# Hybrid decoder step on one core: whole-array products for the chunk scores and the sample tokens, and decays as biases of the exponentials

## The chip, the cores and the metric

The kernel runs on one core of one Trainium2 chip. The metric is the device time of one execution in microseconds. The core's engines work side by side and each takes its own instructions in order: TensorE (PE: matrix products; its weight loads are listed apart as PEld), VectorE (DVE), ScalarE (ACT), GpSimd (POOL), and SyncE (SP), which here only issues transfers. SBUF is the on-chip memory, PSUM the small one in banks of 128 partitions x 512 fp32 that PE writes to.

## The reference, cut to what matters

One layer of a decoder trunk: RMSNorm, one input projection, two groups of heads side by side, one output projection, residual, RMSNorm. 1024 new tokens ("prompt") start from an empty state; 8 sequences of 4 tokens ("sample") start from given states. The group that the change touches is the gated linear recurrence with four heads of 128 keys and 128 values:

```python
def step(s, inp):
    qb, kb, vb, gb = inp
    g = jnp.cumsum(gb, axis=2)                     # summed log of the forget gates
    diff = g[:, :, :, None, :] - g[:, :, None, :, :]
    decay = jnp.exp(jnp.where(causal, diff, -jnp.inf))
    scores = jnp.einsum('nhtd,nhsd,nhtsd->nhts', qb, kb, decay)
    o = (jnp.einsum('nhts,nhsv->nhtv', scores, vb)
         + jnp.einsum('nhtd,nhdv->nhtv', qb * jnp.exp(g), s))
    g_last = g[:, :, -1:, :]
    s_new = (jnp.exp(g_last[:, :, 0, :])[..., None] * s
             + jnp.einsum('nhsd,nhsv->nhdv', kb * jnp.exp(g_last - g), vb))
    return s_new, o
```

Here `k = 1 - f`, `gb = log(f)`, `f = lb + (1 - lb) * sigmoid(...)`. The output of each head goes through an RMSNorm and is gated with `silu(za)`. The other group is a gated depthwise convolution of width 31 with LayerNorm; it runs mostly on DVE.

## The kernel before, in words

Activations lie transposed: 128 channels on the partitions, 1056 tokens (1024 prompt, 32 sample) along the free dimension. `emit` walks over a list `order` of 24 blocks of 128 output channels. For each, `load_w` fetches the weights, ACT rounds them into a high part `wh` and DVE takes the low part `wl`; `project` multiplies them in three column blocks of 352, each with 24 matmuls into one of four `mm` banks. ACT or DVE then empties the banks (`evac`), ACT after a load of the table for the sigmoid or SiLU. All calls on PE and DVE are recorded with one line, L72, since they go through the helper `Clock`.

The recurrence of head `hd` is the generator `hgrn`. It is queued when its q block is projected, and `pump` takes steps from it, and from the convolution's generator `conv`, between the column blocks of later projections. A scheduler then sets the final order on each engine from these priorities and a simulated timeline. The recurrence's small matmuls therefore stand among the projections' on PE, and the convolution's multiply-adds fill DVE.

For the prompt, `hgrn` runs in two halves of 512 tokens, each of four chunks of 128. `base` (L511) subtracts, on DVE, the summed gate at the middle of each chunk, takes two exponentials on ACT (L514, L515) and multiplies them with k and q on DVE. The scores of a chunk are then made in two pieces, in tiles of 64 columns of PE's array (tile names: `ptps` is the score bank, `hw` holds the products with k and q, `pt` the masked scores):

```python
T.matmul(ptps[0:64, cs], lhsT=kb[:, c * P : c1], rhs=qb[:, cs], ...)
T.matmul(ptps[64:P, c1:ce], lhsT=kb[:, c1:ce], rhs=qb[:, c1:ce], ..., tile_position=(0, 64))
```

The quarter above the diagonal is not computed; DVE clears the bank once (L974), and `masked` copies the causal part of the scores into `pt`. k is transposed on PE, copied by ACT (L532), and multiplied with the values `vt` for the state (`aux<-vt,ho`); `ops` takes scores times values plus queries times state. `head_norm` normalizes.

For the sample tokens of each head, `hgrn` lays the decayed keys out four times (`k4`, tile `kts`), transposes them, repeats the head's 32 value rows on four groups of partitions by a product with a constant matrix (`aux<-vs,bones`, 32 rows of the array), forms the 32 x 32 scores from a second set of exponentials in a tile of 32 columns (`aux<-sm`), masks them into `ptss`, and multiplies them with the 32 value rows (`ops<-pts,vs`, 32 rows). `aux<-raw,qz` and `aux<-hw,kts` are the products with the old and for the new states; `raw` holds the state, read and written by SP's queue.

If the decays were too strong for the factored form, a flag that is computed on the way starts a second, slower program (`fast=False`). It does not run on this data.

Of the kernel before, what the change touches and what calls it, by code (L numbers as in the profile page):

```python
# [21 lines left out]
NB = 8  # L22
NS = 4
ST = NB * NS
# [3 lines left out]
H = 4  # L28
# [4 lines left out]
EPS = 1e-6  # L33
LB_MIN = 0.02
RANGE = 60.0
VPOS = 4
LEAD = 10.0
HU = 3
# [7 lines left out]
C_HG = 0  # L46
# [10 lines left out]
NMASK = 2 + len(LEVELS)  # L57
# [39 lines left out]
def emit(nc, tc, h, fast, flag_out=None):  # L97
    HW = 5
    with ExitStack() as ctx:
# [5 lines left out]
        def sb(shape, tag, bufs=1, dt=F32):  # L105
            return pool.tile(shape, dt, tag=tag, name=tag, bufs=bufs)
# [18 lines left out]
        make_identity(nc, ident)  # L125
        eps = sb([P, 1], "eps")
        nc.vector.memset(eps, EPS)
        avgr = sb([P, P], "avg", dt=F32R)
        avg = avgr.bitcast(F32)
        av = sb([P, P], "st", 5)  # L130
# [9 lines left out]
        vs = sb([P, P], "vs")  # L140
# [182 lines left out]
        cols = sb([P, C_END], "cols")  # L323
# [29 lines left out]
        ptss = sb([P, ST], "pts")  # L353
        nc.gpsimd.memset(ptss, 0.0)


        lb = sb([P, 4], "lb")
        omlb = sb([P, 4], "omlb")
        nomlb = sb([P, 4], "nomlb")
# [11 lines left out]
        V.tensor_scalar(nomlb, lb, -1.0, None, ALU.add)  # L371
        if fast:
            rng = sb([P, H, 16], "rng")
        wsum = sb([P, 60], "wsum")
# [87 lines left out]
        def hgrn(hd, q, k, g):  # L462
# [4 lines left out]
            if fast:  # L467

                gc = g[:, 0:SEQ].rearrange("p (c t) -> p c t", t=P)
                r0, r1 = rng[:, hd, 0:8], rng[:, hd, 8:16]  # L470
                V.tensor_copy(r0, gc[:, :, P // 2 - 1])
                V.tensor_tensor(r1, gc[:, :, P - 1], r0, ALU.subtract)

                eg = sb([P, 9], "eg", 2)
                V.tensor_tensor(eg[:, 1:8], r0[:, 1:8], r1[:, 0:7], ALU.add)
                V.tensor_copy(eg[:, 8:9], r1[:, 7:8])
                S.activation(eg[:, 1:9], eg[:, 1:9], AF.Exp)
            for hf in range(2):
# [32 lines left out]
                def base(blk, idx, src=gv, n=512, mk=hw, qq=qv, kk=kv):  # L511
                    d = rel(blk, idx, src, n, mk)
                    kb = mk()
                    S.activation(kb, d, AF.Exp, scale=-1.0)  # L514
                    S.activation(d, d, AF.Exp)  # L515
# [7 lines left out]
                if fast:  # L523


                    qb, kb = base(P, P // 2 - 1)
                    yield
                    kps = aux()
                    for c in range(4):
# [2 lines left out]
                    S.copy(kT, kps)  # L532
                    for c in range(4):
                        cs = slice(c * P, (c + 1) * P)
                        c1, ce = c * P + P // 2, c * P + P

                        T.matmul(
                            ptps[0:64, cs], lhsT=kb[:, c * P : c1], rhs=qb[:, cs],
                            start=True, stop=True,
                        )  # L540
                        T.matmul(
                            ptps[64:P, c1:ce], lhsT=kb[:, c1:ce], rhs=qb[:, c1:ce],
                            start=True, stop=True, tile_position=(0, 64),
                        )
                    for pr in range(2):
                        masked(
                            pts[pr],
# [116 lines left out]
                        stop=True,  # L664
                    )
                yield
                yield from head_norm(hd, c0, 512, ops)
            if fast:
                end = sb([P, P], "st", 5)
                V.tensor_scalar(end, st, eg[:, 8:9], None, ALU.mult)  # L670
                st = end
            nc.sync.dma_start(h["o_hp"][hd], st)
            yield
# [13 lines left out]
            k4 = sb([P, 4, ST], "kts", 3)  # L687
            V.tensor_tensor(
                k4,
                ki.unsqueeze(1).to_broadcast([P, 4, ST]),  # L690
                kv.unsqueeze(1).to_broadcast([P, 4, ST]),
                ALU.mult,
            )
# [16 lines left out]
            for dst, src, r0, r1 in ((kT, 0, 2, 4), (vr, P, 1, 2), (vr, P, 3, 4)):  # L710
                rr = slice(r0 * ST, r1 * ST)
                V.tensor_tensor(
                    dst[rr], kps[rr, src : src + P], dst[rr].bitcast(F32), ALU.subtract
                )
            qi = sm()
            S.activation(qi, gv, AF.Exp)
            qz = qzs[0]
# [4 lines left out]
                ALU.mult,  # L722
            )
            yield
            sps = aux()
            if fast:
                qb, kb = base(NS, 1, gv, ST, sm, qv, kv)
                pairs = [(kb, qb)]
            else:
# [5 lines left out]
            for i, (a, b) in enumerate(pairs):  # L735
                sp = sps[rows, i * ST : (i + 1) * ST]
                T.matmul(sp, lhsT=a, rhs=b, start=True, stop=True, tile_position=(0, hd * ST))
                mi = 0 if fast else NMASK - 3 + i
                V.copy_predicated(ptss[rows, :], smask[rows, mi, :], sp)
            ops = bank("ops", 1)  # L740
            T.matmul(
                ops[:, 0:ST],
                lhsT=vs[rows, :],
                rhs=ptss[rows, :],
                start=True,
                stop=False,
                tile_position=(hd * ST, 0),
            )
            ips = aux()
            for b in range(NB):  # L750
# [6 lines left out]
                    stop=(b >= 4),  # L757
                    tile_position=(0, j * ST),
                )
            isb = sb([P, P], "kts", 3)  # L760
            S.copy(isb, ips[:, 0:P])
            T.matmul(ops[:, 0:ST], lhsT=isb, rhs=bones[:, 0:ST], start=False, stop=True)
            yield
# [20 lines left out]
                    )  # L784
            nc.sync.dma_start(h["o_hs"][hd], so)
            yield
            yield from head_norm(hd, SEQ, ST, ops)
            hdone.add(hd)

        def head_norm(hd, c0, n, ops):  # L790
# [8 lines left out]
            S.activation(r, ms[:, 0:n], AF.Ln, bias=eps)  # L799
            S.activation(r, r, AF.Exp, scale=-0.5)  # L800
            V.scalar_tensor_tensor(
                r, ops[:, 0:n], cols[:, C_HG : C_HG + 1], r, ALU.mult, ALU.mult
            )
            yield

# [161 lines left out]
        for i, (kind, c) in enumerate(order):  # L967
            if i == VPOS:
                t0 = T.ns
                for tb in range(2, 8):  # L970
                    v_block(tb)
                T.ns = t0
                ptps = bank("ptps", 1)
                V.memset(ptps, 0.0)  # L974
                late["ptps"] = ptps
                mixa = late["mixa"] = big()
            if i + 1 < len(order):
# [29 lines left out]
            elif kind == "f":  # L1007
# [2 lines left out]
                project(w, act_into(kt, AF.Sigmoid), nd)  # L1010
                S.activation(g, kt, AF.Ln, bias=lb[:, c : c + 1], scale=omlb[:, c : c + 1])
                S.activation(
                    kt, kt, AF.Identity, bias=omlb[:, c : c + 1], scale=nomlb[:, c : c + 1]
                )
                for hf in range(4):
                    gs = g[:, hf * 256 : hf * 256 + 256]
# [339 lines left out]
```

## Time and profile before

| | us |
|---|---|
| time, median of 3 runs (lowest, highest) | 500.35 (499.99, 501.29) |
| the profiled execution's own time | 500.03 |
| its span, first to last instruction | 498.2 |
| PE busy in the span | 484.2 |
| DVE busy | 358.6 |
| ACT busy | 250.6 |
| PE's granted clock, mean | 0.993 |

By place in the span: up to about 133 us x is normed and transposed, the values of all tokens and the first blocks are projected. From 133 to about 372 us the recurrence of the four heads runs among the projections. From there to 403 come the last gate blocks and LayerNorm, then the output projection up to 489, and the last rows' norm and write.

A row of the timeline has: start in us, length in us, engine, line, operation, output tile <- input tiles, active rows * columns of the array, shape, count, and in brackets the idle time before. Rows of one kind that follow one another are merged, and a row's length reaches to the end of its last matmul, which overlaps the next row; so the distance between starts is the time that something takes on PE.

### The profile page before, as it was taken

What the parts mean: (1) busy time and instruction counts of PE and PEld (TensorE: products, weight loads), DVE (VectorE), ACT (ScalarE), POOL (GpSimd) and SP (SyncE); (2) the same over time, 40 slices, a digit from 0 to 9 for tenths busy, and PEclk for the clock granted to TensorE, in tenths of its full rate; (3) what the DMA queues carried; (4) which work ended last, traced back from release to release, by engine and by line L of the source; (5) the groups of instructions that cost most, each with busy time, mean ns of one, the idle gap of its engine ahead of it and who ended that gap; (6) DMA issues with size and microseconds to landing.
All of it is one profiled execution on the core that took longest, in us unless ns stands there. A gap on an engine that the chain in (4) does not pass through costs nothing.

```text
span 498.2 us, 7600 instructions
## 1 busy us (share of the span) xinstructions
PE 484.2 (97%) x3020; PEld 442.7 (89%) x3020; DVE 358.6 (72%) x682; ACT 250.6 (50%) x439; POOL 3.0 (1%) x20
## 2 busy tenths in 40 slices
PE   6999999999999999999999999999999999999992
PEld 5788899999999998999999999999999977877781
DVE  4864213999999989998999988993677747543441
ACT  5764332413646554635536554545766985422321
POOL 1000000000000000000000000000000000000000
PEclk9999999999999999999999999999999999999997
DMA  7910501231111213211123101131115396432111
GB/s 272 314 43 13 170 25 30 42 62 36 42 44 43 52 49 61 88 43 43 48 55 128 27 27 49 42 128 44 47 43 180 89 415 202 153 114 86 42 53 49
DMA packets 23003, 43.52 MB, mean 87 GB/s; under 512 B 10640, under 2 KB 11920, under 8 KB 22960
## 3 DMA queue, kind: packets, MB, share of 16 engines
q1 hardware_dynamic: 21808, 40.86, 26.3%
q10 hardware_dynamic: 1152, 2.10, 1.1%
q8 instruction: 25, 0.41, 0.3%
q14 instruction: 18, 0.15, 0.1%
HBM read 35.72 MB, written 7.24 MB: 86 GB/s over the span
## 4 chain that ended last, share of the span: by engine, by line
PE 90%; ACT 4%; DMA 3%; DVE 2%; issue 1%; SPq 0%; DVEq 0%
PE mm L72 70%; PE ops L72 8%; PE ptps L72 6%; PE aux L72 5%; DMA u<-gin 1%; ACT big L954 1%; DMA raw<-wo 1%; DMA o_hs<-raw 1%; DVE raw L72 1%; ACT L455 1%; DVE qkg L72 0%; ACT big L1100 0%; DVE big L72 0%; ACT qkg L455 0%; DVE u L72 0%
## 5 line engine op out<-in xcount | busy, mean ns | idle before, releaser
L72 PE MATMUL mm<-big,wh 128*128 128x352 f32 (+1 forms) x1280 | 323.7, 332 | 0.0
L72 PEld LDWEIGHTS mm<-big,wh 128*128 128x128 f32 x1280 | 224.1, 188 | 8.1 <-issue 1.6
L72 PE MATMUL mm<-big,wl 128*128 128x352 f32 (+1 forms) x640 | 211.4, 331 | 0.0
L72 PEld LDWEIGHTS mm<-big,wl 128*128 128x128 f32 x640 | 120.5, 188 | 3.4 <-issue 0.4
L72 DVE TENSOR_TENSOR wl<-wraw,wh 128x1024 fp32r<-128x1024 f32 x24 | 29.3, 1222 | 25.9 <-ACT wh L390 25.8
L72 DVE SCALAR_TENSOR_TENSOR big<-u,wsum,big 128x511 f32<-128x511 f32 (+14 forms) x60 | 44.5, 741 | 0.6
L72 DVE SCALAR_TENSOR_TENSOR big<-u,cols,big 128x511 f32<-128x511 f32 (+14 forms) x60 | 44.0, 735 | 0.0
L72 DVE SCALAR_TENSOR_TENSOR cq<-u,cols,cq 128x511 f32<-128x511 f32 (+13 forms) x56 | 41.2, 735 | 0.0
L72 DVE TENSOR_TENSOR qkg<-mm,big 128x512 f32<-128x512 f32 x16 | 10.9, 690 | 35.7 <-PE mm L72 35.7
L390 ACT CAST wh<-wraw 128x1024 fp32r<-128x1024 f32 x24 | 25.1, 1047 | 17.2 <-issue 7.8
L72 PE MATMUL mm<-vt,wh 128*128 128x512 f32 x64 | 25.6, 402 | 0.4 <-ACT wh L1167 0.4
L395 ACT ACT_TABLE_LOAD x20 | 25.7, 1283 | 0.3
L455 ACT ACTIVATE qkg<-mm 128x352 f32<-128x352 f32 x48 | 19.4, 465 | 11.4 <-PE mm L72 11.3
L72 PE MATMUL mm<-vt,wl 128*128 128x512 f32 x64 | 24.8, 390 | 0.0
L1204 ACT ACTIVATE big<-qkg 128x512 f32<-128x512 f32 x16 | 10.0, 628 | 29.1 <-DVE qkg L72 29.1
L455 ACT ACT_TABLE_LOAD x16 | 20.5, 1283 | 1.3 <-PE mm L72 1.0
L72 PE MATMUL ops<-big 128*128 128x512 f32 x64 | 20.8, 403 | 0.2 <-ACT big L197 0.2
L72 PE MATMUL ptps<-big 128*128 128x512 f32 x64 | 19.9, 394 | 0.0
L1167 ACT CAST wh<-big 128x512 fp32r<-128x512 f32 x16 | 9.2, 617 | 19.1 <-PE mm L72 18.6
L72 PEld LDWEIGHTS mm<-vt,wh 128*128 128x128 f32 x64 | 12.0, 188 | 5.2 <-ACT wh L1167 1.7
L72 PE MATMUL mm<-hw,wh 128*128 128x512 f32 x40 | 15.7, 392 | 0.0
L799 ACT ACTIVATE big<-aux,eps 128x512 f32<-128x512 f32 (+1 forms) x12 | 6.7, 556 | 17.9 <-PE aux L72 17.5
(239 smaller groups left out, 634.7 us busy)
## 6 DMA issues: line engine op xcount, KB each, us to landing
wraw<-win SPq DMA_DIRECT2D x24, 512.0 KB, 3.6
wraw<-wo SPq DMA_DIRECT2D x12, 512.0 KB, 3.7
big<-xp SPq DMA_DIRECT2D x2, 2048.0 KB, 10.1
big<-xp SPq DMA_DIRECT2D x4, 512.0 KB, 10.7
raw<-sh SPq DMA_DIRECT2D x4, 512.0 KB, 3.5
o_hs<-raw SPq DMA_DIRECT2D x4, 512.0 KB, 3.0
raw<-wo SPq DMA_DIRECT2D x4, 512.0 KB, 5.2
o_yp<-qkg ACTq DMA_DIRECT2D x8, 256.0 KB, 2.9
```

The costliest lines, as they stand in the source:

```text
L72: return f(*a, **k)
L390: S.copy(hi, wr)
L395: after(S.preload_act_table_set("natural_log_exp_and_others"), prev)
L455: return [S.activation(dst[:, nb * MB : (nb + 1) * MB], ps, func, bias=bias)]
L799: S.activation(r, ms[:, 0:n], AF.Ln, bias=eps)
L954: return S.activation(cv[:, c, cs], cv[:, c, cs], AF.Silu, bias=cols[:, C_LNB + c : C_LNB + c + 1], scale=cols[:, C_LNG + c : C_LNG + c + 1],)
L1167: S.copy(hv, m[:, :, ts])
L1204: S.activation(xr[:, hs], y[:, hs], AF.Square, accum_out=sqs[:, half : half + 1])
```

## The change

- The scores of a chunk become one whole 128 x 128 x 128 product. The part above the diagonal is computed too and masked away as before. The clearing of the bank goes.
- `base` is no longer used for the prompt. The exponentials read the summed gates directly, chunk by chunk, with the chunk's middle value (`rng`, and its negative `nm`) as the bias of the ACT instruction: 8 instructions of 128 columns per half in place of two of 512 (64 in place of 16 in all).
- k is scaled by 2^-16 where it is made (`kb0`, `kw`); the scale is taken out again in the norm (`hgk`, and a scale in the logarithm), in the final state and in the sample's `k4`.
- The sample scores use the four-fold `k4` as weights of a whole product of 32 columns, behind the transpose in the same bank, and the same exponential for q (`qe`). The scores of a head lie in a plane of their own in `ptss` (zero elsewhere), so that their product with the values is whole as well.
- The repeated value rows come by four transfers on SP's queue per head (`v4`), and are rounded by ACT from there. Tile `kts` has four buffers in place of three.

```diff
+                nm = sb([P, 8], "nm", 2)
+                V.tensor_scalar(nm, r0, -1.0, None, ALU.mult)
...
-                    qb, kb = base(P, P // 2 - 1)
+                    qb, kb = hw(), hw()
+                    for c in range(4):
+                        cs, cc = slice(c * P, (c + 1) * P), hf * 4 + c
+                        S.activation(
+                            kb[:, cs], gv[:, cs], AF.Exp, bias=r0[:, cc : cc + 1], scale=-1.0
+                        )
+                    for c in range(4):
+                        cs, cc = slice(c * P, (c + 1) * P), hf * 4 + c
+                        S.activation(qb[:, cs], gv[:, cs], AF.Exp, bias=nm[:, cc : cc + 1])
+                    V.tensor_tensor(kb, kb, kv, ALU.mult)
+                    V.tensor_tensor(qb, qb, qv, ALU.mult)
...
-                        T.matmul(
-                            ptps[0:64, cs], lhsT=kb[:, c * P : c1], rhs=qb[:, cs],
-                            start=True, stop=True,
-                        )
-                        T.matmul(
-                            ptps[64:P, c1:ce], lhsT=kb[:, c1:ce], rhs=qb[:, c1:ce],
-                            start=True, stop=True, tile_position=(0, 64),
-                        )
+                        T.matmul(ptps[:, cs], lhsT=kb[:, cs], rhs=qb[:, cs], start=True, stop=True)
...
+            v4 = sb([P, P], "kts", 4)
+            for j in range(4):
+                nc.sync.dma_start(v4[j * ST : (j + 1) * ST, :], vs[rows, :])
+            yield
...
+            if fast:
+                qe = sm()
+                S.activation(qe, ki, AF.Exp)
+                V.tensor_tensor(qe, qe, qv, ALU.mult)
...
-            T.matmul(
-                kps[:, P : 2 * P],
-                lhsT=bones[rows, :],
-                rhs=vs[rows, :],
-                start=True,
-                stop=True,
-                tile_position=(hd * ST, 0),
-            )
-            kT = sb([P, P], "kts", 3, F32R)
-            vr = sb([P, P], "kts", 3, F32R)
+            if fast:
+                sps = kps[:, P : P + ST]
+                T.matmul(
+                    sps, lhsT=k4.rearrange("p a t -> p (a t)"), rhs=qe, start=True, stop=True
+                )
+                V.copy_predicated(ptss[rows, hd, :], smask[rows, 0, :], sps[rows, :])
+            vr = sb([P, P], "kts", 4, F32R)
+            S.copy(vr, v4)
+            kT = sb([P, P], "kts", 4, F32R)
             S.copy(kT, kps[:, 0:P])
-            S.copy(vr, kps[:, P : 2 * P])
...
             T.matmul(
                 ops[:, 0:ST],
-                lhsT=vs[rows, :],
-                rhs=ptss[rows, :],
+                lhsT=vs,
+                rhs=ptss[:, hd, :],
                 start=True,
                 stop=False,
-                tile_position=(hd * ST, 0),
             )
...
-                V.memset(ptps, 0.0)
```

Since the scheduler sets the order, these rows show what moves. A row is a line, an operation, output tile <- input tiles and the output's shape; a count stands at the end. First PE at the scores of the first head's first half (`mm` is a projection, `aux<-ident,hw` the transposes of k), before and then after:

```order
L72 MATMUL aux<-ident,hw 128x128 x4
L72 MATMUL mm<-big,wh 128x352 x2
L72 MATMUL mm<-big,wl 128x352
...
L72 MATMUL ptps<-hw 64x128
L72 MATMUL ptps<-hw 64x64
...
L72 MATMUL mm<-big,wh 128x352 x2
L72 MATMUL mm<-big,wl 128x352
...
L72 MATMUL aux<-vt,ho 128x128 x4
```

```order
L73 MATMUL aux<-ident,hw 128x128 x4
L73 MATMUL mm<-big,wh 128x352
L73 MATMUL mm<-big,wl 128x352
...
L73 MATMUL mm<-big,wh 128x352
L73 MATMUL ptps<-hw 128x128 x4
L73 MATMUL mm<-big,wh 128x352
L73 MATMUL mm<-big,wl 128x352
```

Eight pieces of two widths, alternating, become four products of one shape in the same place between the projections.

PE at the first head's sample tokens, without the projections between the rows, before and after:

```order
L72 MATMUL aux<-ident,kts 128x128
L72 MATMUL aux<-vs,bones 128x128
...
L72 MATMUL aux<-sm 32x32
...
L72 MATMUL aux<-raw,qz_425 32x128 x8
...
L72 MATMUL ops<-pts,vs 128x32
L72 MATMUL aux<-hw,kts 128x512
...
L72 MATMUL ops<-bones,kts 128x32
L72 MATMUL aux<-hw,kts 128x512
```

```order
L73 MATMUL aux<-ident,kts 128x128
L73 MATMUL aux<-sm,kts 128x32
...
L73 MATMUL aux<-raw,qz_425 32x128 x8
...
L73 MATMUL ops<-pts,vs 128x32
...
L73 MATMUL aux<-hw,kts 128x512
...
L73 MATMUL ops<-bones,kts 128x32
L73 MATMUL aux<-hw,kts 128x512
```

The repeat of the value rows is gone from PE, and the score product has moved up behind the transpose; the others keep their sequence.

ACT between two emptyings of projections (`qkg<-mm`: q of the first head, then the forget gates of the second), before and after:

```order
L390 CAST wh<-wraw 128x1024
L514 ACTIVATE hw<-hw 128x512
L686 ACTIVATE sm<-sm 128x32
L514 ACTIVATE sm<-sm 128x32
L515 ACTIVATE hw<-hw 128x512
L515 ACTIVATE sm<-sm 128x32
L477 ACTIVATE eg<-eg 128x8
L532 COPY ho<-aux 128x512
L455 ACT_TABLE_LOAD
```

```order
L397 CAST wh<-wraw 128x1024
L538 ACTIVATE hw<-qkg,rng 128x128 x4
L704 ACTIVATE sm<-sm 128x32
L735 ACTIVATE sm<-qkg 128x32
L543 ACTIVATE hw<-qkg,nm 128x128 x4
L486 ACTIVATE eg<-eg 128x8
L706 ACTIVATE sm<-sm 128x32
L728 CAST kts<-kts 128x128
L538 ACTIVATE hw<-qkg,rng 128x128 x4
L543 ACTIVATE hw<-qkg,nm 128x128 x4
L462 ACT_TABLE_LOAD
```

The two wide exponentials of one half have become eight narrow ones, the second half's eight stand ahead of the same table load too, and the copy `ho<-aux` has moved behind it.

More of the change, by code (lines that the diff above doesn't have):

```diff
@@ L35 @@
 RANGE = 60.0
+KS = 2.0 ** -16
 VPOS = 4
@@ L127, in emit @@
         nc.vector.memset(eps, EPS)
+        ks = KS if fast else 1.0
         avgr = sb([P, P], "avg", dt=F32R)
@@ L352, in emit @@
         nc.sync.dma_start(bones, h["bones"])
-        ptss = sb([P, ST], "pts")
+        ptss = sb([P, H, ST], "pts")
         nc.gpsimd.memset(ptss, 0.0)
@@ L358, in emit @@
         omlb = sb([P, 4], "omlb")
-        nomlb = sb([P, 4], "nomlb")
+        kc = sb([P, 9], "kc")
+        kb0, kw, hgk = kc[:, 0:4], kc[:, 4:8], kc[:, 8:9]
         l0 = cols[:, C_LOG : C_LOG + 4]
@@ L370, in emit @@
         V.tensor_scalar(omlb, lb, -1.0, 1.0, ALU.mult, ALU.add)
-        V.tensor_scalar(nomlb, lb, -1.0, None, ALU.add)
+        V.tensor_scalar(kb0, lb, -ks, ks, ALU.mult, ALU.add)
+        V.tensor_scalar(kw, lb, ks, -ks, ALU.mult, ALU.add)
+        V.tensor_scalar(hgk, cols[:, C_HG : C_HG + 1], 1.0 / ks, None, ALU.mult)
         if fast:
@@ L666, in hgrn @@
                 yield
-                yield from head_norm(hd, c0, 512, ops)
+                yield from head_norm(hd, c0, 512, ops, ks, hgk)
             if fast:
                 end = sb([P, P], "st", 5)
-                V.tensor_scalar(end, st, eg[:, 8:9], None, ALU.mult)
+                V.tensor_scalar(end, st, eg[:, 8:9], 1.0 / ks, ALU.mult, ALU.mult)
                 st = end
@@ L724, in hgrn @@
             yield
[L725 to L729, printed above, removed]
+            if not fast:
+                sps = aux()
                 pairs = []
@@ L734, in hgrn @@
                 pairs.append((kv, qv))
[L735 to L739, printed above, removed]
+                for i, (a, b) in enumerate(pairs):
+                    sp = sps[rows, i * ST : (i + 1) * ST]
+                    T.matmul(sp, lhsT=a, rhs=b, start=True, stop=True, tile_position=(0, hd * ST))
+                    V.copy_predicated(ptss[rows, hd, :], smask[rows, NMASK - 3 + i, :], sp)
             ops = bank("ops", 1)
@@ L759, in hgrn @@
                 )
-            isb = sb([P, P], "kts", 3)
+            isb = sb([P, P], "kts", 4)
             S.copy(isb, ips[:, 0:P])
@@ L786, in hgrn, with head_norm @@
             yield
-            yield from head_norm(hd, SEQ, ST, ops)
+            yield from head_norm(hd, SEQ, ST, ops, 1.0, cols[:, C_HG : C_HG + 1])
             hdone.add(hd)
-        def head_norm(hd, c0, n, ops):
+        def head_norm(hd, c0, n, ops, ks, hg):
             lo = sb([P, 512], "ho", 2, F32R)
@@ L798, in head_norm @@
             mean(ms[:, 0:n], hi[:, 0:n], lo[:, 0:n])
-            S.activation(r, ms[:, 0:n], AF.Ln, bias=eps)
+            S.activation(r, ms[:, 0:n], AF.Ln, bias=eps, scale=1.0 / (ks * ks))
             S.activation(r, r, AF.Exp, scale=-0.5)
             V.scalar_tensor_tensor(
-                r, ops[:, 0:n], cols[:, C_HG : C_HG + 1], r, ALU.mult, ALU.mult
+                r, ops[:, 0:n], hg, r, ALU.mult, ALU.mult
             )
@@ L1012, in emit @@
                 S.activation(
-                    kt, kt, AF.Identity, bias=omlb[:, c : c + 1], scale=nomlb[:, c : c + 1]
+                    kt, kt, AF.Identity, bias=kb0[:, c : c + 1], scale=kw[:, c : c + 1]
                 )
```

13 lines of the change are left out of this document (6 added, 7 removed).

## The prediction

> **What bounds the kernel now.** I read the page's busy times first, then the chain that ended last, then the busy times by stretch. The page's engine line and the chain's shares:
>
> ```profile
> PE 484.2 (97%) x3020; PEld 442.7 (89%) x3020; DVE 358.6 (72%) x682; ACT 250.6 (50%) x439; POOL 3.0 (1%) x20
> PE 90%; ACT 4%; DMA 3%; DVE 2%; issue 1%; SPq 0%; DVEq 0%
> ```
>
> TensorE is at work almost from end to end, but its busy time is modelled and an average, so the stretches matter. Columns: stretch; us and busy us (instructions) of PE, weight loads, DVE, ACT, POOL; granted clock; DMA share; GB/s.
>
> ```profile
> 133.00:160.00 27.00, 27.00 (x186) 26.59 (x185) 25.94 (x55) 15.05 (x26) 0.00 (x0) 1.00 0.15 40
> 160.00:215.00 55.00, 55.00 (x389) 51.83 (x389) 50.90 (x102) 29.79 (x49) 0.25 (x2) 1.00 0.25 67
> 215.00:270.00 55.00, 55.00 (x374) 52.75 (x372) 52.15 (x106) 29.36 (x50) 0.00 (x0) 1.00 0.18 53
> 270.00:330.00 60.00, 60.00 (x416) 57.83 (x416) 55.25 (x108) 31.20 (x53) 0.00 (x0) 1.00 0.18 55
> 330.00:372.00 42.00, 42.00 (x295) 40.02 (x293) 26.73 (x45) 24.78 (x39) 0.00 (x0) 1.00 0.18 56
> ```
>
> All that the change touches lies between 133 and 372 us. There PE never stops and has its full clock, so a TensorE slot that goes away shortens the run by its own length, as long as nothing else takes over. DVE is the nearest: 25.94 + 50.90 + 52.15 + 55.25 = 184.2 us of the 197 up to 330, or 93.5%. ACT has 130.2 of 239 us.
>
> **Chunk scores.** PE around the first head's first half. Every fp32 product shows as two MATMULs.
>
> ```profile
> 146.50 0.32 PE L72 MATMUL mm<-big,wl 128*128 128x352 f32 x1
> 146.75 1.09 PE L72 MATMUL ptps<-hw 128*64 128x128 f32 x16
> 147.77 0.59 PE L72 MATMUL mm<-big,wh 128*128 128x352 f32 x2
> 148.20 0.32 PE L72 MATMUL mm<-big,wl 128*128 128x352 f32 x1
> 148.36 0.48 PE L72 MATMUL mm<-big,wh 128*128 128x352 f32 x2
> 148.68 0.32 PE L72 MATMUL mm<-big,wl 128*128 128x352 f32 x1
> 148.84 1.05 PE L72 MATMUL aux<-vt,ho 128*128 128x128 f32 x8
> ...
> 150.05 0.32 PE L72 MATMUL mm<-big,wl 128*128 128x352 f32 x1
> ```
>
> A projection matmul starts every 0.16 us (three from 148.20 to 148.68). The cost of a group is the time between the projection matmuls around it, less these themselves. The scores in 64-column tiles take 148.20 - 146.50 - 3 x 0.16 = 1.22 us. The group at 148.84 is four whole 128x128x128 products, exactly the shape that the scores will have: 150.05 - 148.68 - 0.48 = 0.89 us, or 0.11 per MATMUL. What the tiles lose is at their edges: the group starts 0.25 after the matmul ahead instead of 0.16, and the two behind take 0.43 instead of 0.32.
>
> The rule that speaks against this edit is in the Trainium skill, TensorEngine Tiling, section Theoretical Speedup: a dimension of 64 or less may run up to 2x faster in tiles. By that alone the whole products would cost up to twice the tiled group, an estimate of +1.22 us per half and +9.8 in all. The same page's Key Properties say that a change of tiling mode drains the array; the two gaps in the rows above agree with that.
>
> Six of the eight halves have one unbroken group and save 0.33 us each: 2.0 us. Two are broken up by whole-array work and have more edges; these are the projection matmuls around them:
>
> ```profile
> 207.36 0.32 PE L72 MATMUL mm<-big,wl 128*128 128x352 f32 x1
> 210.97 0.32 PE L72 MATMUL mm<-big,wl 128*128 128x352 f32 x1
> ...
> 332.75 0.32 PE L72 MATMUL mm<-big,wh 128*128 128x352 f32 x1
> 335.74 0.48 PE L72 MATMUL mm<-big,wh 128*128 128x352 f32 x2
> ```
>
> PE's timeline has in both the 16 score MATMULs, ten whole ones (1.11 us) and some projections. 210.97 - 207.36 = 3.61 with three projections (0.48) leaves 2.02 for the scores: 1.13 saved against 0.89. 335.74 - 332.75 = 2.99 with two (0.32) leaves 1.56: 0.67 saved. Chunk scores together: 2.0 + 1.1 + 0.7 = **-3.8 us**. In the new order some groups are again broken, but whole products among whole products have no edge.
>
> **Sample tokens.** PE in the first head's sample part:
>
> ```profile
> 184.24 0.27 PE L72 MATMUL aux<-ident,kts 128*128 128x128 f32 x1
> 184.44 0.48 PE L72 MATMUL aux<-vs,bones 32*128 32x128 f32 x2
> ...
> 185.12 0.32 PE L72 MATMUL mm<-big,wl 128*128 128x352 f32 x1
> ...
> 189.38 0.32 PE L72 MATMUL mm<-big,wh 128*128 128x352 f32 x1
> 189.63 0.25 PE L72 MATMUL aux<-sm 128*32 128x32 f32 x2
> ...
> 190.07 0.33 PE L72 MATMUL mm<-big,wl 128*128 128x352 f32 x1
> ...
> 193.24 0.32 PE L72 MATMUL mm<-big,wl 128*128 128x352 f32 x1
> 193.49 0.40 PE L72 MATMUL ops<-pts,vs 32*128 32x32 f32 x2
> 193.83 0.50 PE L72 MATMUL aux<-hw,kts 128*128 128x512 f32 x1
> ...
> 195.29 0.30 PE L72 MATMUL ops<-bones,kts 128*128 128x32 f32 x2
> 195.42 0.47 PE L72 MATMUL aux<-hw,kts 128*128 128x512 f32 x1
> ```
>
> - The repeat of the token rows (vs,bones) goes: 185.12 - 184.24, less one projection (0.16) and the transpose, a single MATMUL with its edge (0.14), is 0.58 us; in four heads 2.3.
> - The tiled score (sm) goes: 190.07 - 189.38 less two projections is 0.37. In the last head it sits among the tiled state products and costs next to nothing; three heads give 1.1.
> - The value product (pts,vs) becomes whole: 193.83 - 193.24 - 0.16 = 0.43 ahead of aux<-hw,kts. The whole 32-column pair at 195.29 takes 0.13 ahead of the same product. 0.30 each, 1.2.
> - Added: a whole score product of 32 columns. No row has it behind a transpose. Its bounds are 0.13 (that pair) and 0.22 (a 128-column pair, 2 x 0.11); an added TensorE slot cannot gain. I take 0.2, nearer to the pair that also loads 128 fresh columns of weights for a bank of its own: +0.8.
>
> Together: -2.3 - 1.1 - 1.2 + 0.8 = **-3.8 us**.
>
> **Exponentials and small edits.** Groups by form, then two rows of ACT's timeline:
>
> ```profile
> L72 DVE TENSOR_TENSOR hw<-qkg 128x512 f32<-128x512 f32 x8 | 5.5, 683 | 0.0
> L455 ACT ACTIVATE qkg<-mm 128x352 f32<-128x352 f32 x48 | 19.4, 465 | 11.4 <-PE mm L72 11.3
> L880 ACT ACTIVATE u<-mm,cols 128x352 f32<-128x352 f32 x8 | 4.0, 563 | 0.0
> 138.39 0.62 ACT L515 ACTIVATE hw<-hw 128x512 f32<-128x512 f32 x1
> 138.91 0.21 ACT L515 ACTIVATE sm<-sm 128x32 f32<-128x32 f32 x1
> ```
>
> Sixteen 512-wide exponentials become 64 of 128 with a bias column. The wide one holds ACT for 0.52 us (138.39 to 138.91). Between 0.21 us at 32 columns and 0.62 at 512, a line gives 0.29 at 128; the bias column adds 563 - 465 = 98 ns; the overlap of 0.62 - 0.52 = 0.10 comes off. So 0.30 each, or 0.20 if the bias costs nothing; I take 0.30, since the bias costs it in the row. 64 x 0.30 - 16 x 0.52 = +10.9 us on ACT, then 141 of 239. It lies beside PE's work; what it costs without that cover is rival 2. DVE loses the eight subtractions (5.5 us); the other edits on it (sample subtraction and product, clearing of the score bank, four negations of 8 columns) are left at nothing. With 5.5 less in a stretch 7.6 shorter, DVE has 178.7 of 189.4 us, 94%: as close as before, and no closer, so it does not take over. The rescalings are factors inside instructions that exist and cost nothing.
>
> The four copies per head in place of the repeat go through SP's queue. Rows of SP's and ACT's timelines:
>
> ```profile
> 194.72 0.33 SPq L387 DMA_DIRECT2D wraw<-win  x1
> ...
> 205.15 1.28 ACT L455 ACT_TABLE_LOAD   x1
> 206.44 1.18 ACT L455 ACTIVATE qkg<-mm 128x352 f32<-128x352 f32 x3
> ```
>
> Four issues at 0.33 are 1.3 us of SP. Behind them wait the write and read of the state and later weights. In the second head they stand right behind the load at 194.72, and ACT rounds their rows ahead of the table load at 205.15, ten us later. Between nothing and 1.3 us in each of three heads I take nothing, for that distance.
>
> **Sum.** -3.8 - 3.8 = -7.6 us. The profiled execution took 500.03 us (498.2 of span, 1.8 around it), 0.3 below the median of 500.35, so 492.4 by its own time and 500.35 - 7.6 = 492.75 as a median: **492.7 us**. At the unbroken price for all eight halves (-2.6) and with the dear score product the sum is -6.3 (494.0); with the cheap one -7.9 (492.4). With a microsecond on either side for waits that move, the forecast's own range is 491.4 to 495.
>
> **Rivals.**
> 1. *The slots go, but PE now waits in places.* The score bank is single, and the new order puts transposes, copy and state product at other distances. For it: DVE at 94%. Against: PE waited nowhere in these stretches before. One DVE instruction of 0.68 us waited for in four to six halves costs 2.7 to 4.1: 495.4 to 496.8.
> 2. *ACT comes late to the evacuations, and it gets slower.* A project uses three of four banks; the next one needs the first of them back 24 x 0.16 = 3.8 us after the last matmul. ACT gives it after the table load (1.28) and two evacuations of 1.18 / 3: 2.1 us. So there is 1.7 us of room. In ACT's new order the first head has all 16 exponentials (4.8 us) ahead of one table load. If such a pile could only start with the last matmul, in all four heads, PE would stand 3.1 us each: +12.4, or 505. It decides from 7.6 / 4 + 1.7 = 3.6 us late per head. Against: the pile is in one head, and ACT stays idle 98 us of 239.
> 3. *Tiles pay after all*: whole scores at twice the tiled group, +9.8 in place of -3.8, with the sample's -3.8: +6.0, or 506. The rows at 148.84 are against it. The Trainium skill's section named above is the rule for it.
> 4. *The end is held by something else*, so that nothing arrives. The chain of waits has one candidate behind the last sample part:
>
> ```profile
> 371.93 0.67 PE ops L72 x4
> 375.65 3.27 DMA o_hs<-raw
> ```
>
> It starts at PE, after all the savings, and should move up with them; if it stood still the time would be 500.
>
> **How the numbers follow.** Forecast 0.80, rival 1 0.10, rival 2 0.04, rival 3 0.02, rival 4 0.04. About 0.3% (1.5 us) is what a measurement of this kernel can tell from no change. Faster: 0.80 + 0.10 = 0.90; same 0.04; slower 0.06. The range 491 to 497 takes in the forecast's own range and rival 1.
>
> **What would show it.** Right: PE busy near 476.6; score groups as eight 128*128 MATMULs at about 0.11 each; no 32*128 rows left; DVE some 5 to 7 us lower, ACT about 11 higher. Wrong: holes in PE between 133 and 370 put down to ACT or DVE (rivals 1 and 2), score rows further apart than 0.11 (3), or a PE that reaches its last projection 7 us earlier and then stands (4).

## The result, and the profile after

| | before | after |
|---|---|---|
| time, median (lowest, highest), us | 500.52 (499.99, 501.29) | 493.91 (493.09, 494.13) |
| the profiled execution's own time | 500.03 | 493.09 |
| its span | 498.2 | 491.3 |
| PE, DVE, ACT busy | 484.2, 358.6, 250.6 | 476.7, 353.2, 260.0 |

The ratio is 0.9861, with a 95% interval of 0.9845 to 0.9878: 6.1 to 7.8 us off. The forecast was 492.7.

From the page of the changed kernel, the busy times:

```profile
PE 476.7 (97%) x2948; PEld 441.4 (90%) x2948; DVE 353.2 (72%) x671; ACT 260.0 (53%) x483; POOL 3.2 (1%) x20
```

The time by stretch, with the columns of the prediction's table (stretch; us and busy us of PE, weight loads, DVE, ACT, POOL; granted clock; DMA share; GB/s):

```profile
133.00:365.00 232.00, 232.00 (x1582) 228.88 (x1581) 207.51 (x406) 141.17 (x262) 0.25 (x2) 1.00 0.20 58
365.00:405.00 40.00, 39.69 (x214) 35.53 (x214) 26.27 (x42) 31.80 (x47) 0.00 (x0) 1.00 0.63 227
```

Nothing makes PE wait inside the heads: it is busy 232.00 of 232.00 us at full clock. The stretch behind them lacks only 0.31 us. One of the two groups of exponentials by form (the other, with `nm` as bias, is L543), and PE's timeline around the first scores:

```profile
L538 ACT ACTIVATE hw<-qkg,rng 128x128 f32<-128x128 f32 x32 | 10.3, 394 | 13.5 <-PE ops L73 13.5
```

```profile
147.21 0.32 PE L73 MATMUL mm<-big,wh 128*128 128x352 f32 x1
147.37 1.05 PE L73 MATMUL ptps<-hw 128*128 128x128 f32 x8
148.18 0.41 PE L73 MATMUL mm<-big,wh 128*128 128x352 f32 x1
148.42 0.32 PE L73 MATMUL mm<-big,wl 128*128 128x352 f32 x1
```

The scores are eight whole MATMULs. They begin 0.16 us behind the projection ahead, without an edge. From that projection at 147.21 to the one at 148.42, less the two themselves (0.32), the group costs 0.89 us, the price that was forecast. The exponentials are the 64 short ones.

PE's busy time fell by 7.5 us, the span by 6.9. The difference of about 0.7 us lies before anything that was changed. PE's timeline at the start, before and after:

```profile
5.64 1.46 PE L72 MATMUL mm<-avg 128*128 128x128 f32 x6
8.20 0.63 PE L72 MATMUL mm<-ident,raw 128*128 128x128 f32 x4 [1.10 <-DVE raw L72]
```

```profile
5.73 0.72 PE L73 MATMUL mm<-avg 128*128 128x128 f32 x5
8.24 0.63 PE L73 MATMUL mm<-ident,raw 128*128 128x128 f32 x4 [1.79 <-DVE raw L73]
```

The warm-up products happened to end sooner in the second execution, and PE then waited 0.69 us longer for the same rows of x: 8.20 and 8.24 us. So some 0.7 us of busy time turned into waiting there. The change itself took 6.9 us out.

### The profile page after: what moved, and what is told of

Read it like the earlier page. It is cut to its first block, busy times and chain, and to the rows that moved or that the text cites. A ratio compares the mean times of both kernels' runs of the same rounds, so it can differ in the third digit from the quotient of the medians.

```text
span 491.3 us, 7533 instructions
## 1 busy us (share of the span) xinstructions
PE 476.7 (97%) x2948; PEld 441.4 (90%) x2948; DVE 353.2 (72%) x671; ACT 260.0 (53%) x483; POOL 3.2 (1%) x20
## 4 chain that ended last, share of the span: by engine, by line
PE 92%; DMA 3%; DVE 2%; ACT 1%; issue 0%; SPq 0%; DVEq 0%
PE mm L73 73%; PE ops L73 8%; PE ptps L73 6%; PE aux L73 5%; DMA o_hs<-raw 1%; DMA u<-gin 1%; DMA raw<-wo 1%; DVE raw L73 1%; DVE qkg L73 0%; DVE u L73 0%; ACT L462 0%; DVE big L73 0%; ACT vt L1113 0%; DVE hw L73 0%; ACT big L200 0%
## 5 line engine op out<-in xcount | busy, mean ns | idle before, releaser
L73 DVE TENSOR_TENSOR qkg<-mm,big 128x512 f32<-128x512 f32 x16 | 10.9, 689 | 36.1 <-PE mm L73 36.1
L538 ACT ACTIVATE hw<-qkg,rng 128x128 f32<-128x128 f32 x32 | 10.3, 394 | 13.5 <-PE ops L73 13.5
L894 ACT ACTIVATE u<-mm,cols 128x352 f32<-128x352 f32 (+2 forms) x16 | 6.5, 484 | 17.6 <-PE mm L73 17.6
```

Source lines behind the costliest of these rows:

```text
L73: return f(*a, **k)
L538: S.activation(kb[:, cs], gv[:, cs], AF.Exp, bias=r0[:, cc : cc + 1], scale=-1.0)
L894: out.append(S.activation(dst, src, func, bias=bias))
```

## Experiments: each part alone

**Chunk scores alone.** The kernel before with whole scores (and the factor 2^-16, here in k's product), the exponentials and the samples as they were:

```diff
-                        T.matmul(ptps[0:64, cs], lhsT=kb[:, c * P : c1], rhs=qb[:, cs], ...)
-                        T.matmul(ptps[64:P, c1:ce], ..., tile_position=(0, 64))
+                        T.matmul(ptps[:, cs], lhsT=kb[:, cs], rhs=qb[:, cs], start=True, stop=True)
```

> The kernel before with the chunk scores as whole products and nothing else of the change (the factor 2^-16 sits in the product with k on VectorE here, in one instruction of the same width; exponentials and sample tokens as before). Theory (TensorE slots alone set the time, the tiles lose at their edges): PE busy 484.2 - 3.8 = 480.4, time 500.5 - 3.8 = 496.7. Rival (tiles run two products at once, so the whole ones are dearer, and the gain came from the rest of the change): no gain, 500 or more.

Measured 497.64 us, ratio 0.9934 (0.9917 to 0.9952): 3.3 us off, between 2.4 and 4.2. PE busy 480.8.

**Sample tokens alone.** The changed kernel with the chunk part (tiles, wide exponentials, clearing) as before:

> The changed kernel with the chunk scores in the old 64-column tiles and the old wide exponentials: what is left of the change is the sample part and the copies on SP's queue. Theory: PE busy 480.4, time 496.7, and this gain and that of the whole scores alone add up to that of the whole change. Rival (the sample part hides behind other work): 500.5, and whole scores alone give all.

Measured 497.31 us, ratio 0.9920 (0.9901 to 0.9939): 4.0 us off, between 3.1 and 5.0. The two parts add up to 1.46%; the whole change has 1.39%.

**Exponentials alone, and all but the exponentials.** One run puts only the biased exponentials into the kernel before. The other takes only them out of the changed kernel:

```diff
-                    qb, kb = base(P, P // 2 - 1)
+                    qb, kb = hw(), hw()
+                    for c in range(4):
+                        S.activation(kb[:, cs], gv[:, cs], AF.Exp, bias=r0[:, cc : cc + 1], scale=-1.0)
+                    ...
```

> The kernel before with only the exponentials changed: 64 narrow ones with a bias column on ScalarE, no subtraction on VectorE; scores in tiles, sample tokens as before. Theory: TensorE has the same work and ScalarE has room, so ACT busy rises by 10 to 15 us, DVE falls by 5.5 and the time stays within 1 us of 500.5. Rival (VectorE at 94% was the hidden bound, its 5.5 us are the gain): 495 to 498. Rival (ScalarE late at the evacuations): 502 or more.

> The changed kernel with only the exponentials put back to two wide ones and the subtraction. Theory: the exponentials are worth nothing either way, 493.9 with at most 0.5 to either side. Rival (the 0.7 us that the change fell short of its sum were lost to ScalarE's 10 us more): 493.2 or less. Rival (VectorE's relief carried part of the gain): 496 or more.

Both missed. The first took 504.45 us, ratio 1.0061 (1.0044 to 1.0078), slower than before. The second took 501.42 us, ratio 1.0004 (0.9990 to 1.0018): without the biased exponentials the whole gain was gone, though PE has the changed kernel's 2948 MATMULs. Neither sign fits a price of the exponentials themselves: putting them in costs 3 us in one kernel, and taking them out costs 7.5 in the other. Both have a hole in PE (a stretch in which PE stands still) at one place, behind the last projections. PE's timeline, of the first run and then of the second:

```profile
407.36 0.80 PE L72 MATMUL mm<-vt,wh 128*128 128x512 f32 x1 [2.89 <-ACT wh L1179]
```

```profile
393.33 0.66 PE L73 MATMUL ptps<-cq,avg 128*128 128x352 f32 x1 [4.60 <-ACT cq L939]
395.63 0.80 PE L73 MATMUL mm<-vt,wh 128*128 128x512 f32 x1 [1.64 <-ACT wh L1168]
```

PE waits for ACT: in the first run for the rounded operand of the output projection (`wh`), in the second for that and, before it, for the rounded operand of LayerNorm's last variance product (`cq`).

**Scores twice, exponentials twice.** The changed kernel with one line repeated each time (the same values are computed again):

> The changed kernel with every whole score product made twice into the same place: 64 more MATMULs of 0.11 us on TensorE, nothing else. Theory (each TensorE slot counts in full): +7.1 us, 501.0. Rival (part of TensorE's time is cover, the end is held elsewhere): less than +4.

> The changed kernel with each of the 64 narrow exponentials made twice: 64 x 0.30 = 19 us more on ScalarE in the stretch of 230 us where it is busy 141. Theory (ScalarE is covered there): at most +1 us, 493.9 to 494.9. Rival (ScalarE is late at the evacuations already): +5 or more.

Scores twice: 505.38 us, ratio 1.0089 (1.0075 to 1.0103), where 501.0 was expected. Exponentials twice: 507.32 us, ratio 1.0141 (1.0126 to 1.0156), 13.4 us above the changed kernel, where nothing was expected. Again one hole each: 2.89 us in the first, and in the second

```profile
397.87 1.22 PE L73 MATMUL ptps<-cq,avg 128*128 128x352 f32 x2 [10.83 <-ACT cq L955]
```

These two do not price a score or an exponential as meant, since they changed the order behind the last head as well.

**Tiles.** The changed kernel with all scores in two tiles of 64 columns side by side, both 128 wide, so that the tiles stream a third more than those of the kernel before; and with only one of each half's four chunks in such tiles:

```diff
-                        T.matmul(ptps[:, cs], lhsT=kb[:, cs], rhs=qb[:, cs], start=True, stop=True)
+                        T.matmul(ptps[0:64, cs], lhsT=kb[:, c * P : c1], rhs=qb[:, cs], ...)
+                        T.matmul(ptps[64:P, cs], lhsT=kb[:, c1:ce], rhs=qb[:, cs], ..., tile_position=(0, 64))
```

> The changed kernel with all chunk scores as two products in 64-column tiles again, but both 128 columns wide, so that the two tiles stream as many columns as the whole product does if they run side by side. Theory (side by side; only the edges cost): +0.36 us per half and a bit more where a group is broken, +2.9 to +4, 496.8 to 498. Rival (the tiles run one after the other): +2.9 and another 8 x 0.43, 500 or more.

> The changed kernel with one of four chunks in each half as two 128-wide products in 64-column tiles, the other three whole. Theory (a tiled group costs its two edges whatever its length): as much as all four in tiles, +2.9 to +4, 496.8 to 498. Rival (tiles cost by the product): a quarter of that, +0.7 to +1.

496.73 us, ratio 0.9925 (0.9910 to 0.9940), and 497.54 us, ratio 0.9938 (0.9925 to 0.9951). PE is busy 480.7 and 480.9 us against 476.7, but 15.63 and 15.47 us of that, against 14.88, lie in the first 20 us, where nothing was changed. Behind them PE is busy 0.41 us more per half with four chunks tiled, and 0.45 with one. The first group's rows agree: between the projections around it, less these themselves, it costs 1.23 us with four chunks tiled (147.11 to 148.66) and 1.24 with one (147.30 to 148.86), against 0.89 whole. What tiles cost here is going in and coming out; how much stands between hardly counts.

## Experiments: the order behind the last head

What was left to explain now lay in the stretch from 365 to 405 us. ACT takes its work there in the order that the scheduler fixed: the last head's norm (Ln, Exp), LayerNorm (Square, Ln, Exp), the last gate projections (SiLU), and the roundings for the output projection. SiLU and Ln/Exp need different tables, and each change loads one. In the changed kernel the norm of the last head's sample tokens (L813, L814) stands ahead of the load for the gate projections:

```profile
371.24 0.29 ACT L813 ACTIVATE big<-aux,eps 128x32 f32<-128x32 f32 x1 [1.33 <-PE aux L73]
371.56 0.23 ACT L814 ACTIVATE big<-big 128x32 f32<-128x32 f32 x1
377.72 1.28 ACT L462 ACT_TABLE_LOAD   x1
```

In the kernel before it does too (379.65 and 379.97, the load at 385.31). ACT's timeline in the run that lost the gain (the changed kernel with wide exponentials):

```profile
375.49 1.28 ACT L462 ACT_TABLE_LOAD   x1
376.79 1.18 ACT L462 ACTIVATE qkg<-mm 128x352 f32<-128x352 f32 x3
...
382.55 1.28 ACT L801 ACT_TABLE_LOAD   x1
383.84 0.29 ACT L801 ACTIVATE big<-aux,eps 128x32 f32<-128x32 f32 x1
...
386.36 1.28 ACT L462 ACT_TABLE_LOAD   x1
387.66 0.47 ACT L462 ACTIVATE qkg<-mm 128x352 f32<-128x352 f32 x1
388.14 1.28 ACT L802 ACT_TABLE_LOAD   x1
389.44 0.23 ACT L802 ACTIVATE big<-big 128x32 f32<-128x32 f32 x1
389.68 1.28 ACT L462 ACT_TABLE_LOAD   x1
...
392.79 0.49 ACT L939 CAST cq<-u 128x352 fp32r<-128x352 f32 x1
```

The same norm, 0.29 and 0.23 us of work on 32 columns (L801, L802 here), stands behind the first gate projections. That costs four table loads, 5.1 us, ahead of the rounding at 392.79 for which PE stands 4.60 us.

In the run with the biased exponentials in the kernel before, another pair is split. The samples' norm stands ahead as it should, but LayerNorm's last Ln and Exp (L953, L954) alternate with the last SiLUs (L455):

```profile
389.45 1.28 ACT L953 ACT_TABLE_LOAD   x1
...
391.32 1.28 ACT L455 ACT_TABLE_LOAD   x1
...
393.10 1.28 ACT L954 ACT_TABLE_LOAD   x1
...
394.91 1.28 ACT L455 ACT_TABLE_LOAD   x1
```

From the first load for the last gate projections (381.90) to the rounding that PE waits for (406.69), this run has eight table loads; the kernel before has four (385.31 to 401.94), so four more here as well. The scores issued twice have the same eight.

Four runs tell an order from a price. The first keeps the wide exponentials and only schedules that norm at high priority:

```diff
-            yield from head_norm(hd, SEQ, ST, ops, 1.0, cols[:, C_HG : C_HG + 1])
+            with tc.high_priority(HP):
+                for _ in head_norm(hd, SEQ, ST, ops, 1.0, cols[:, C_HG : C_HG + 1]):
+                    pass
+            yield
```

> The changed kernel with wide exponentials, as in the run that lost the whole gain (501.4 us), and with one thing more: the norm of the samples' outputs (Square, Ln, Exp on 32 columns) is scheduled at high priority, which puts the last head's Ln and Exp ahead of the last gate projections on ScalarE and takes three of ScalarE's table loads (1.28 us each) out of the stretch before the output projection. Theory: the order there cost the 7.5 us. Four table loads of the chain ahead of LayerNorm's last rounding go with Ln and Exp (4 x 1.28 + 0.52 = 5.6 us, more than PE's hole of 4.60 us), so the hole shrinks below 1.5 us, the granted clock there stays at 0.97 or above, and the time is 493.5 to 496.5 us. Rival: the wide exponentials cost it wherever they stand (VectorE's subtractions and multiplies being later): 500.5 to 502 us, hole or not.

492.82 us, ratio 0.9842 (0.9821 to 0.9863). The whole gain is back, and more of it than expected. ACT's timeline at the same place, and PE's stretch:

```profile
374.36 0.29 ACT L804 ACTIVATE big<-aux,eps 128x32 f32<-128x32 f32 x1 [0.70 <-PE aux L73]
...
374.92 1.28 ACT L462 ACT_TABLE_LOAD   x1
...
387.01 0.49 ACT L942 CAST cq<-u 128x352 fp32r<-128x352 f32 x1 [0.17 <-DVE u L73]
```

```profile
365.00:405.00 40.00, 40.00 (x219) 36.37 (x218) 27.87 (x47) 30.39 (x50) 0.00 (x0) 1.00 0.64 227
```

Norm first, then one table load; the rounding comes 5.8 us sooner, and PE no longer waits. The changed kernel itself has 493.91 us, and the intervals overlap, so with this order the biased exponentials are worth nothing that these runs can tell. (No run has both the biased exponentials and the norm's high priority, so a small effect of each against the other is not excluded.)

The second has the biased exponentials in heads 0 to 2 of the kernel before, where the order behind the last head stays that of before:

```diff
-                    qb, kb = base(P, P // 2 - 1)
+                    if hd < 3:
+                        qb, kb = hw(), hw()
+                        ...
+                    else:
+                        qb, kb = base(P, P // 2 - 1)
```

> The kernel before with the biased exponentials in heads 0 to 2 and the wide ones in head 3, chosen because the order of ScalarE's work behind the last head is then again that of the kernel before (one batch of sigmoid-linear projections, then LayerNorm's Ln). Theory: the 0.61% that the biased exponentials cost alone came from the order behind the last head, not from the exponentials. Then 500.1 to 501.3 us, no hole over 0.6 us in PE before 482 us, granted clock 0.99 or above. Rival: each head's biased exponentials cost their share of it. Then three quarters of 3.1 to 3.6 us are lost: 502.9 to 503.4 us.

500.88 us, ratio 1.0000 (0.9987 to 1.0012); one hole is slightly over the 0.6 us that was expected at most, 0.67 us behind ACT at 387.17. Three quarters of the exponentials cost nothing.

The last two repeat exponentials in the changed kernel, in head 0 and in heads 0 and 1 (the same values again):

```diff
-                    for c in range(4):
+                    for c in [i for i in range(4) for _ in range(2 if hd < 1 else 1)]:
```

> The changed kernel with head 0's sixteen biased exponentials issued twice (16 more, same values, 4.8 to 6.3 us of ScalarE's time); the order behind the last head is that of the changed kernel. Theory: 493.5 to 494.7 us, since nobody waits for ScalarE inside the heads and the order behind them is unchanged. Rival: the repeated exponentials of all four heads cost 13.4 us by themselves; a quarter of that is 3.4 us: 497.3 us.

> As the run before with heads 0 and 1 (32 more exponentials). Here the scheduler puts the last head's Ln and Exp behind the last gate projections, each with a table load of its own. Theory: 500 to 507 us, with a hole of 3 to 10 us in PE behind the last projections and the first 330 us of the span as in the changed kernel; the step from one head to two is many times that from none to one. Rival: twice a quarter of 13.4 us, 500.6 us, spread over the heads, with no hole behind the last projections.

Head 0: 493.64 us, ratio 0.9855 (0.9835 to 0.9875), the changed kernel's time. Heads 0 and 1: 499.21 us, ratio 0.9961 (0.9949 to 0.9973), just under what was expected; the rival's 500.6 would fit as well. The step tells them apart: sixteen more exponentials cost nothing, the next sixteen 5.6 us, where the rival has equal shares. And the holes are behind the last head. PE's timeline there, and ACT's table loads ahead of it:

```profile
390.24 0.43 PE L73 MATMUL ptps<-cq,avg 128*128 128x352 f32 x1 [1.85 <-ACT cq L951]
392.19 0.66 PE L73 MATMUL ptps<-cq,avg 128*128 128x352 f32 x1 [1.52 <-DVE cq L73]
393.48 0.80 PE L73 MATMUL mm<-vt,wh 128*128 128x512 f32 x1 [0.63 <-ACT wh L1180]
394.08 0.63 PE L73 MATMUL mm<-hw,wh 128*128 128x512 f32 x1
394.50 0.63 PE L73 MATMUL mm<-vt,wh 128*128 128x512 f32 x1
...
400.71 0.39 PE L73 MATMUL mm<-hw,wh 128*128 128x512 f32 x1
400.94 0.39 PE L73 MATMUL mm<-vt,wl 128*128 128x512 f32 x1
```

```profile
383.46 1.28 ACT L813 ACT_TABLE_LOAD   x1
386.00 1.28 ACT L814 ACT_TABLE_LOAD   x1
387.54 1.28 ACT L462 ACT_TABLE_LOAD   x1
```

These runs in one table, each against the kernel that has the same MATMULs. By 133 us, ahead of all recurrence work, all of them have started the same 778 MATMULs except two, which have 768: from 15 to 20 us the clock was 0.85 and 0.83 in those two executions, where the changed kernel has 1.00. Ten MATMULs of 0.16 us are a late start of some 1.6 us, which has nothing to do with the order.

| run | holes behind the last projections, us | span | span over its kernel | of that longer holes, late start | rest |
|---|---|---|---|---|---|
| before | 0.41 | 498.2 | | | |
| before, biased exponentials | 2.89 | 502.7 | +4.5 | 2.5, 0 | 2.0 |
| after | 0.30 | 491.3 | | | |
| after, wide exponentials | 4.60 and 1.64 | 499.8 | +8.5 | 5.9, 1.6 | 1.0 |
| the same, norm ahead | none | 490.2 | -1.1 | -0.3, 0 | -0.8 |
| exponentials twice, head 0 | 0.31 | 491.2 | -0.1 | 0.0, 0 | -0.1 |
| twice, heads 0 and 1 | 1.85, 1.52, 0.63 | 498.6 | +7.3 | 3.7, 1.6 | 2.0 |
| twice, all heads | 10.83 | 505.0 | +13.7 | 10.5, 0 | 3.2 |

Holes explain most, but not all. The rest of 1.0 to 3.2 us in the four rows with long holes goes with PE's clock, which drops in the hole and stays low behind it (last section); that share is a remainder, not measured by itself. The -0.8 of the run with the norm ahead lies behind the last head too: from 133 to 365 us both kernels start 1582 MATMULs, and from there to 405 that run starts 219, the changed kernel 214. Scores twice fits as well: of its +12.4 us of span (503.7), the 64 repeated products are 64 x 0.11 = 7.0 us and the longer hole is 2.6, which leaves 2.8.

What stays open is why the scheduler turns the order over. The runs show that a few more or fewer instructions in the heads are enough, and that the order, not those instructions, costs the time.

## Why the prediction was right, and where it was not

- **The sum.** Forecast -7.6 us. The span fell by 6.9, the median by 6.6, and the interval (6.1 to 7.8) holds it. "PE busy near 476.6" was met by 476.7, but 0.7 us of that is the start-up, so this sign was right partly by luck.
- **Chunk scores, -3.8.** Alone they gave -3.3 (2.4 to 4.2), which holds the forecast. The mechanism stands: an unbroken group costs 0.89 us with no edge in front, and tiles lose at their edges whether four chunks are tiled or one. The step that looked weakest is the two broken halves (1.13 and 0.67), since broken groups remain in the new order. The rows bear it out. PE around one of them in the changed kernel:

```profile
271.60 0.32 PE L73 MATMUL mm<-big,wl 128*128 128x352 f32 x1
...
271.98 1.06 PE L73 MATMUL aux<-vt,ho 128*128 128x128 f32 x8
...
273.46 0.57 PE L73 MATMUL mm<-big,wh 128*128 128x352 f32 x2
273.87 0.33 PE L73 MATMUL mm<-big,wl 128*128 128x352 f32 x1
```

From 271.60 to 273.87, less three projections (0.48) and the eight MATMULs `aux<-vt,ho` (0.89), the eight score MATMULs cost 0.90 us: a group of whole products that is broken by other whole products costs no more than an unbroken one. What the run alone lacks to 3.8 is inside its interval, and no row places it.
- **Sample tokens, -3.8.** Alone -4.0 (3.1 to 5.0). The added score product was put at 0.2 us and took 0.14, near its lower bound; the other terms were not taken apart by any run. The sign "no 32*128 rows left" holds for the products of the recurrence; eight MATMULs of 32*128 elsewhere (`mm<-ident,qkg`, `aux<-ident,qkg`) stay. PE in the first head's sample part:

```profile
192.11 0.27 PE L73 MATMUL aux<-ident,kts 128*128 128x128 f32 x1
192.22 0.30 PE L73 MATMUL aux<-sm,kts 128*128 128x32 f32 x2
192.36 0.57 PE L73 MATMUL mm<-big,wh 128*128 128x352 f32 x2
```

- **Exponentials, 0.** ACT rose by 9.4 us where +10.9 was worked out, DVE fell by 5.4 where 5.5 was, and in the heads nobody waited. As a price the zero holds: three heads of them 1.0000, sixteen more 493.64, none of them 492.82. What failed is the reasoning for it. The cover named was ACT's idle time up to 372 us. The place where ACT has no room is behind that. In the kernel before PE already waited for it there:

```profile
402.61 0.50 PE L72 MATMUL mm<-vt,wh 128*128 128x512 f32 x1 [0.41 <-ACT wh L1167]
```

There the edit's effect is not ACT's added time but the order in which the scheduler puts a Ln and an Exp of half to one microsecond together (the samples' norm or LayerNorm's), and their table loads. The zero came true in the changed kernel because its order there is the good one; one edit to either side it is not. That part was luck.
- **SP's copies, 0.** They are in the sample run, which gave its full 4.0 us.
- **Rival 1** (PE waits inside the heads) fell: 232.00 of 232.00. **Rival 2** (ACT late to the evacuations) fell at its place, with the pile of 16 exponentials doubled in head 0 at no cost. **Rival 3** (tiles pay) fell. Tiles do run side by side: with all chunks tiled, the 16 half-array MATMULs of the first group take 1.02 us (147.37 to 148.39), 0.06 each, where the eight whole ones take 0.81, 0.10 each. But the edges leave no gain in groups of 0.9 us. The Trainium skill (TensorEngine Tiling (Array Packing), Theoretical Speedup) gives up to 2x for a dimension of 64 or less; no run here shows a gain from tiles.
- **Rival 4** (the end is held by something else) was given 0.04 and the place was right, not the way. It was written as a chain that starts at PE and moves up with it. It is ACT's order, and five of the twelve runs made with small edits fell into it, with 4.5 to 13.7 us more span than they should have had (1.6 of it a late start in two of them) or, for the scores issued twice, 5.4 more than their work. The chance was too small, and the step that sized it took one order as given.

## What to carry to other kernels

Where a scheduler fixes the order of an in-order engine, look for the stretch in which that engine is nearly as late as the bound one, and count its table loads there: an edit elsewhere that costs nothing by itself can turn that order over and cost more than the edit gains. An experiment that repeats or removes work must first be looked at for what else moved; two kernels that share the order of the tight stretch are what can be compared. A short group of half-array products among whole ones is paid for at its edges, here with 0.34 us a group; whether a longer group would pay, no run shows.

## What the hardware showed that was not expected

PE's granted clock halved in a hole of 2.89 us, about 2 us after the hole began, and stayed so for some 6 us after work resumed. By stretch, in the kernel before with biased exponentials (hole from 404.47 to 407.36):

```profile
404.00:406.00 2.00, 0.47 (x3) 0.04 (x1) 0.52 (x1) 1.97 (x3) 0.00 (x0) 1.00 1.02 412
406.00:408.00 2.00, 0.64 (x2) 0.55 (x3) 0.66 (x2) 1.82 (x3) 0.00 (x0) 0.62 1.02 406
408.00:410.00 2.00, 2.00 (x6) 1.63 (x5) 1.26 (x3) 1.04 (x1) 0.00 (x0) 0.50 1.04 414
410.00:412.00 2.00, 2.00 (x6) 1.54 (x5) 0.60 (x1) 0.00 (x0) 0.00 (x0) 0.50 0.89 272
412.00:414.00 2.00, 2.00 (x8) 1.59 (x7) 0.00 (x0) 0.00 (x0) 0.00 (x0) 0.68 0.64 225
```

At half clock a 512-column MATMUL of the output projection starts every 0.42 us (394.08 to 394.50 above) in place of 0.23 (400.71 to 400.94). The Trainium skill (TensorE: Matmul & The Clock Gate, Part 1: The HAM clock gate) has the clock halve after at least one idle window of about 3.4 us. Here 2.89 us was enough (in the run with the scores twice too), and in the run with heads 0 and 1 repeated it was 4.0 us in three pieces with single MATMULs between them; where the Trainium skill and these rows differ, the rows decide: less than that window can do. The holes of 0.3 to 0.7 us in the other runs left the clock at 1.00. In between, the length of one hole did not decide: at the start of the span a wait of 1.79 us left the changed kernel's clock at 1.00 in the first 20 us, and with a wait of 1.46 us at the same place the run with the norm ahead had 0.91. So the 2.89 us hole cost 4.5 in all: 2.5 more of waiting than before, and 2.0 that are left for slower work behind it.

A table load took 1.28 us and no more. In the run with wide exponentials, the last ACTIVATE ahead of the load at 382.55 ends at 382.53, and the Ln starts 1.29 us after the load does (383.84). The Trainium skill (ScalarE: Activation LUTs, What ACT_TABLE_LOAD costs) adds a drain of about 1.38 us for each switch; no row here shows it.
